# A data-dependent branch moved in a fused two-block transformer: its tiles, its place, and the loads ahead of it

## The chip, the cores and the metric

The kernel runs on one core of a Trainium2 chip. The metric is the device time of one execution in microseconds, the median of several runs. The engines are TensorE (PE, its weight loads PEld), VectorE (DVE), ScalarE (ACT), GpSimd (POOL) and SyncE (SP), which here issues the weight transfers.

## The reference

One sequence of 256 tokens with 1024 features, float32, goes through two blocks. The first block is a layer norm, an adaptive modulation, a mixing layer (latent attention beside an RWKV recurrence) and a mixture of experts; the second block is two layers of feed-forward, mixing (three kinds of heads) and feed-forward. The change touches the mixture of experts alone:

```python
logits = (ht @ router_w + router_b)
top_val, top_idx = lax.top_k(logits, 4)            # 4 of 32 experts for each token
gates = jax.nn.softmax(top_val, axis=-1)
u = clamped_swiglu(h_rows @ w1[e] + b1[e])         # w1[e]: 1024 x 2048
y = u @ w2[e] + b2[e]                              # w2[e]: 1024 x 1024
out[token] += gate * y
```

Every expert has a row count that depends on the data; 256 tokens by 4 choices over 32 experts are 32 rows in the mean.

## The kernel before, in words

The program is unrolled. A scheduler that works from a timeline simulation puts the instructions of each engine in order ahead of time; each engine then runs its own list and waits on semaphores. Instructions inside a conditional block are not mixed with those outside it.

The experts are worked in 16 pairs (`moe`, line 1255 and on). Each expert has 64 slots, so that a pair fills 128 rows. For each pair `gather` (L1152 and on) builds a one-hot of the pair's tokens (`oh`, VectorE), its gated form (`go`, GpSimd), picks the rows on TensorE (16 matmuls `m<-oh,xx`), evicts them into `xg` (VectorE and ScalarE in turn) and transposes `go` into `GT`. Then come the first layer (`p` or `s` `<-w,xg`, in two halves f of 1024 columns), transposes and the clamped SwiGLU into `u0` and `u1`, the second layer (`<-w,u`), the scaling into `y`, and the product of `GT` and `y` (`m<-y,GT`) that is added to `acc`. The gather of pair pr + 1 is written between the first and the second layer of pair pr, and the scheduler places it earlier still.

The weights come in 1 MB tiles: 16 of the first layer and 8 of the second for each pair, 24 x 16 = 384 in all, each by one SyncE transfer (`wtile`, L158). They go to buffers of 2 rings with 6 and 10 buffers, which the mixture of experts uses as one ring of 16 (`slot_tile`, L161): tile i waits until the users of tile i - 16 are done. A tile of the first layer may be loaded ahead (`prefetch`). SyncE's transfers take eight semaphores (lanes) in turn, named DMAHW0 to DMAHW7 in the order. After the experts `block2_buffers` takes buffers of the same rings for the second block, and loads and splits the first feed-forward weights.

An expert may be chosen by more than 64 tokens. `router` keeps the largest count in `over`; `moe_rest` holds a branch (`values_load` L1344, `tc.If` L1345) that is entered only where `over` is above 64, and then works every expert over all tokens. The branch stands ahead of pair 4, and its working tiles are four buffers of the ring:

```python
if pr == 4:
    self.prefetch(pr, 11)
    self.moe_rest()
```

Of the kernel before, what the change touches and what calls it, by code (L numbers as in the profile page):

```python
# [26 lines left out]
RING2 = 10  # L27
MAGIC = 12582912.0
# [5 lines left out]
# ---------------------------------------------------------------- constants  # L34
def const_arrays():
    """Arrays that depend on shapes alone: identity, masks, selections, frequencies."""
# [6 lines left out]
    a["zero"] = np.zeros((128, 128), f)   # ahead of the causal mask: queries of the second tile  # L43
# [28 lines left out]
def const_arrays2():  # L72
# [9 lines left out]
    perm = np.zeros((128, 128), f)        # [source, destination]  # L82
# [25 lines left out]
# the turns of a mixing layer: tiles of the input projection and streams of work  # L108
# [3 lines left out]
# the turns of the first block's streams of work  # L112
# [3 lines left out]
class K:  # L116
# [12 lines left out]
    # ------------------------------------------------------------ helpers  # L129
# [5 lines left out]
    def banks(self, ctx, **tags):  # L135
        """PSUM banks by stream; streams with banks of their own can run ahead of one another."""
        self.psp = ctx.enter_context(self.tc.tile_pool(name="ps", bufs=1, space=PSUM))
        self.psn = tags
# [22 lines left out]
    def slot_tile(self, which=0):  # L161
        """The next 1 MB buffer of the weight stream; in the mixture of experts it has both rings."""
        if self.ring_i is not None:
            which = int(self.ring_i % (RING + RING2) >= RING)
            self.ring_i += 1
        return self.t(self.rings[which], [128, 2048], "w")

    def rsqrt(self, pool, x, n, scale=1.0, eps=0.0, floor=None, tag="rs", eng=None):
        """x [128, n] -> 1/sqrt(x * scale + eps), three Newton steps on the vector engine."""
# [20 lines left out]
    def split(self, hi, lo, src, hi_eng="s", lo_eng="v"):  # L190
        """src (float32) = hi + lo exactly, both of the short float32r form."""
        nc = self.nc
        if hi_eng == "s":
            nc.scalar.copy(hi, src)  # L194
        elif hi_eng == "v":
            nc.vector.tensor_copy(hi, src)
        else:
            nc.gpsimd.tensor_copy(hi, src)
        (nc.vector if lo_eng == "v" else nc.gpsimd).tensor_tensor(lo, src, hi, op=OP.subtract)  # L199
# [7 lines left out]
    def conv_slot(self, w, ring=1, n=1024, **kw):  # L207
        """[128, n] of weights, split into a buffer of a ring."""
# [10 lines left out]
    def bcast_T(self, out, col):  # L219
        """out[p, t] = col[t, 0] for t in the 128 partitions of col."""  # L220
        self.mm(out, col.to_broadcast([128, 128]), self.ident)

    # ------------------------------------------------------------ block 1
# [14 lines left out]
    def load_rows(self, name, items, pool, queues):  # L238
        """Rows of 128 from the small vectors."""
# [7 lines left out]
    def to_cols(self, name, rows, pool):  # L247
        """Rows of 128 to columns over the partitions."""
# [7 lines left out]
    def phase_a(self, ctx):  # L256
# [6 lines left out]
        # ---- first loads  # L263
# [31 lines left out]
        # ---- silu(c), spread to 32 columns for the matrix-vector products  # L295
# [9 lines left out]
        # ---- embedding layer norm (tokens on partitions), transposed  # L305
# [27 lines left out]
        # ---- h = LN(x) (1 + scale) + shift by chunks of features, each as soon as its columns of the modulation are  # L333
        # there, and the rows of w_in that meet it (the columns of RWKV), into seven banks
# [40 lines left out]
        # token shift  # L375
# [5 lines left out]
        # residual alpha * x, features on partitions, in place  # L381
# [90 lines left out]
        # the streams of work and the order in which they take turns  # L472
# [12 lines left out]
        # residual and layer norm 1 (tokens on partitions), logits of the router from the sums before the norm  # L485
# [62 lines left out]
    def ln_stats2(self, pool, parts):  # L548
        """Of two token tiles: (mean, variance) [128, 2, 2], 1 / sqrt(variance + eps) and minus mean times that [128, 2]."""
# [17 lines left out]
    def matvec(self, p, w):  # L567
        """Four partial sums of silu(c) @ w in rows 0, 32, 64, 96 of p."""
# [4 lines left out]
    def ada_pair(self, j, ws):  # L573
        """Columns 2 j, 2 j + 1 of the first two sections of modT, [128, 48] = silu(c) @ ada_w + ada_b."""
# [12 lines left out]
    def ada_tile(self, sec, j, w, tag):  # L587
        """Columns 2 j, 2 j + 1 of a section of modT."""
# [10 lines left out]
    def mla(self, M, ml, sq, qlat, kvl, krot, cosT, sinT, wqn, wqr, wuk, wuv):  # L599
        """Latent attention: norms, rotary parts, values.  # L600
        Yields after every group of matrix products that the vector engines have to follow."""
# [7 lines left out]
        # rms norms of the two latents  # L609
# [22 lines left out]
        # rotary parts  # L632
# [29 lines left out]
    def mla_heads(self, ml, cs, tag, n, oT):  # L662
        """Two heads for each chunk in cs: operands [96, 2, T], scores, softmax, values."""
# [54 lines left out]
    def mla_end(self, ml, oT):  # L718
# [5 lines left out]
        # rms norm over all heads  # L724
# [16 lines left out]
    def softmax(self, t, e, p, H, S_, scale, mask):  # L741
        """p [128, H * S_] scores in PSUM -> normalised rows in SBUF."""
# [15 lines left out]
    def rwkv(self, hh, tag, wa, wg):  # L758
        """RWKV-7 for the four heads of channel chunks 2 hh and 2 hh + 1; the result replaces r in Z.
        Yields after every group of matrix products that the vector engines have to follow."""  # L760
# [7 lines left out]
        # twelve working pieces of [128, 512], in three of the weight stream's buffers  # L768
        bufs = [self.slot_tile(1) for _ in range(3)]
        raw = lambda i: bufs[i // 4][:, (i % 4) * 512:(i % 4) * 512 + 512]  # L770
        q2 = lambda i: raw(i).rearrange("p (c t) -> p c t", c=2)                    # features on partitions
        n4 = lambda i: raw(i).rearrange("p (a h s) -> p a h s", a=2, h=4)           # tokens on partitions
# [9 lines left out]
        # decay and in-context rate  # L782
# [19 lines left out]
        # kk = normalised k * k_k ; k' = k (1 + (a - 1) k_a)  # L802
# [36 lines left out]
        def blocks(lhs, rhs, par, p, o0=0):  # L839
            # [64, 64] per (tile, head, chunk parity) on partitions parity * 64 + row;  # L840
            # the two head parities are two row tiles of the array: a bank for each
# [15 lines left out]
        # inverse of I + strictly lower, by doubling of the diagonal blocks, 32 wide  # L857
# [11 lines left out]
        def coupling(n):  # L869
            # the rows of level n that couple the halves of its diagonal blocks  # L870
# [21 lines left out]
        RbkT = bufs[0][:, 1024:2048].rearrange("p (x s) -> p x s", s=64)            # b and b1 are spent  # L892
# [3 lines left out]
        def others():  # L896
            # the rest of the operands, between the steps of the inverse
# [15 lines left out]
            # tokens-on-partitions copies: [128, tile, 4 heads, 64]  # L913
# [24 lines left out]
        # last doubling to 64: X = V22 A21 V11  # L938
# [12 lines left out]
        # Y0 = A_ak V  # L951
# [15 lines left out]
        # chunk by chunk: U = -T (kk S^T + Y0) ; S^T <- e^bC S^T + a^ U + k^ V  # L967
# [35 lines left out]
        # outputs, tokens on partitions, group norm per head  # L1003
# [26 lines left out]
        # back to features on partitions; affine, bonus, gate  # L1030
# [21 lines left out]
    # ------------------------------------------------------------ mixture of experts  # L1052
    def row_of(self, out, cols, k0, n):
        """out[p, 128 i + j] = cols[j, k0 + i] on every partition (PSUM)."""
# [3 lines left out]
    def router_prep(self, Ro):  # L1058
        """h = xn1 * A2 + B2; router weights scaled by A2 with their column sums, and the constant part of the logits."""
# [25 lines left out]
    def router(self, Ro, plg, mv, rs, space):  # L1085
        """Top 4 of 32, gates, slot of every token in each of its experts; space: two of [128, 256]."""
# [59 lines left out]
    def one_hot(self, oh, pr):  # L1146
        """Of a pair of experts: oh[t, a, (expert, slot)] = 1 where the token sits."""
# [4 lines left out]
    def gather(self, Mo, pr):  # L1152
        """Rows of a pair of experts: xg [128 d, 8, (expert, slot)] and the gated one-hot [(expert, slot), T]."""
# [26 lines left out]
        else:  # L1180
            # the first pair takes its rows as they come
# [16 lines left out]
    def swiglu_clamped(self, gl, ln, th, pg, pl, bg, bl, u, flat=lambda x: x):  # L1198
        """u = 2 * min(g, 7) sigmoid(1.702 min(g, 7)) (clip(l, -7, 7) + 1), g and l in PSUM plus biases."""
# [9 lines left out]
    def moe_bias1(self, Mo):  # L1209
        """First-layer biases as columns: [j, (glu 8 | lin 8), expert]."""  # L1210
# [9 lines left out]
    def moe_base(self, Mo):  # L1220
        """The sum over experts starts as alpha * x1 + (1 + gt2) * (gates @ b2), tokens on partitions."""
# [34 lines left out]
    def moe(self, Mo, B):  # L1256
# [6 lines left out]
        for pr in range(self.pairs):  # L1263
            if pr == 4:
                self.prefetch(pr, 11)
                self.moe_rest()
# [34 lines left out]
            if pr + 1 < N_EXP // 2:  # L1301
                nxt = self.gather(Mo, pr + 1)
            last = pr == N_EXP // 2 - 1
            if last:
                # the sum so far goes ahead into the banks that take the last pair's part
# [18 lines left out]
            for a in range(2):  # L1324
                for d in range(2):
# [5 lines left out]
                    V.tensor_tensor(o, o, p, op=OP.add)  # L1331

    def moe_rest(self):
        """Tokens past an expert's 64 slots: every expert over all tokens, gated; only entered when there are any."""
# [4 lines left out]
        u, h2T = r3(self.slot_tile(), 8), r3(self.slot_tile(), 8)  # L1339
        wt, tm = self.slot_tile(), self.slot_tile()  # L1340
        tmps = [tm[:, i * T:(i + 1) * T] for i in range(4)]
        og, sel, bc = r3(tm[:, 1024:1088], 2), r3(tm[:, 1088:1152], 2), r3(tm[:, 1152:1168], 8)
        cnt, gc = tm[:, 1168:1169], tm[:, 1169:1171]
        rv = nc.values_load(self.over[0:1, 0:1], min_val=0, max_val=T)  # L1344
        with tc.If(rv > SLOTS):  # L1345
            for k in range(8):
# [3 lines left out]
                V.tensor_scalar(h2T[:, k], p[:, :T], self.A2[:, k:k + 1], self.B2[:, k:k + 1], op0=OP.mult, op1=OP.add)  # L1350
            V.scalar_tensor_tensor(og, self.slot, SLOTS - 0.5, self.gate, op0=OP.is_gt, op1=OP.mult)
            V.memset(cnt, 0.0)
            with tc.For_i(0, N_EXP, 1) as e:
# [6 lines left out]
                for f in range(4):  # L1360
                    ph = [ps("p") for _ in range(2)]
                    for k in range(8):
                        w = wt[:, (k % 2) * 512:(k % 2) * 512 + 512]
                        nc.sync.dma_start(w, I["exp_w1"][0, bass.ds(e, 1), k * 128:(k + 1) * 128, f * 512:(f + 1) * 512].rearrange("o p c -> p (o c)"))
                        for j in range(2):
                            for s in range(2):
                                mm(ph[j][:, s * T:(s + 1) * T], w[:, j * 256 + s:(j + 1) * 256:2], h2T[:, k], k == 0 and s == 0, k == 7)
                    for j in range(2):
                        c_ = f * 2 + j
                        self.swiglu_clamped(*tmps[:3], ph[j][:, :T], ph[j][:, T:], bc[:, c_, 0:1].to_broadcast([128, T]),  # L1370
# [558 lines left out]
```

## Time and profile before

| | us |
|---|---|
| median of 3 runs | 2356.72 |
| lowest and highest run | 2351.95, 2367.12 |
| span of the profiled execution | 2349.5 |
| PE busy | 2273.6 (97%) |
| DVE busy | 1174.8 (50%) |
| ACT busy | 719.5 (31%) |
| POOL busy | 159.8 (7%) |
| weights of the experts | 384 transfers of 1024 KB |

The span goes from the first to the last instruction of one profiled execution; for that execution no device time is given apart from its span. Matmul ends are modelled, so a busy TensorE is not one at its peak. A matmul in float32 appears as two records. The trace shows none of the instructions inside the branch: with the inputs used here it is not entered.

### The profile page before, as it was taken

What the parts mean: (1) busy time and instruction counts of PE and PEld (TensorE: products, weight loads), DVE (VectorE), ACT (ScalarE), POOL (GpSimd) and SP (SyncE); (2) the same over time, 40 slices, a digit from 0 to 9 for tenths busy, and PEclk for the clock granted to TensorE, in tenths of its full rate; (3) what the DMA queues carried; (4) which work ended last, traced back from release to release, by engine and by line L of the source; (5) the groups of instructions that cost most, each with busy time, mean ns of one, the idle gap of its engine ahead of it and who ended that gap; (6) DMA issues with size and microseconds to landing.
All of it is one profiled execution on the core that took longest, in us unless ns stands there. A gap on an engine that the chain in (4) does not pass through costs nothing.

```text
span 2349.5 us, 37821 instructions
## 1 busy us (share of the span) xinstructions
PE 2273.6 (97%) x15957; PEld 1641.7 (70%) x15957; DVE 1174.8 (50%) x2233; ACT 719.5 (31%) x1186; POOL 159.8 (7%) x189
## 2 busy tenths in 40 slices
PE   7999899999999999999997999999999999999998
PEld 6777643343344434333334999999999999999998
DVE  5758332221222222212214666896667666897664
ACT  4423111110000000000003444654444444655443
POOL 3310100000000000000002000120001000121000
PEclk9879999999999999999999999999999999999999
DMA  9625899999999999999997554534555655535550
GB/s 322 187 74 187 312 397 383 391 403 362 399 408 401 406 408 407 409 408 409 409 409 275 198 183 159 180 108 146 186 190 163 197 180 162 180 102 169 188 188 19
DMA packets 275967, 626.46 MB, mean 267 GB/s; under 512 B 14576, under 2 KB 160368, under 8 KB 275760
## 3 DMA queue, kind: packets, MB, share of 16 engines
q1 hardware_dynamic: 274240, 621.38, 72.4%
q8 instruction: 127, 2.08, 0.4%
q0 software_dynamic: 1264, 2.08, 0.3%
q10 hardware_dynamic: 288, 0.52, 0.1%
q14 instruction: 48, 0.39, 0.0%
HBM read 622.89 MB, written 1.05 MB: 266 GB/s over the span
## 4 chain that ended last, share of the span: by engine, by line
PE 67%; DMA 8%; DVE 2%; ACT 1%; issue 0%; DVEq 0%; ACTq 0%
PE p L148 22%; PE s L148 21%; PE m L148 15%; DMA w<-in_exp_w_dram 8%; PE r L148 8%; PE r L1288 1%; DVE w L199 0%; PE r L1289 0%; ACT w L1489 0%; DVE w L1490 0%; PE s L1728 0%; PE m L1195 0%; DVE xx L1525 0%; DVE l2y L178 0%; DVE l2x L179 0%
## 5 line engine op out<-in xcount | busy, mean ns | idle before, releaser
L199 DVE TENSOR_TENSOR w<-w,w 128x1024 fp32r<-128x1024 f32 (+2 forms) x360 | 439.3, 1229 | 265.7 <-ACT w L194 265.7
L194 ACT CAST w<-w 128x1024 fp32r<-128x1024 f32 (+2 forms) x364 | 375.2, 1041 | 455.2 <-PE m L148 254.1
L148 PE MATMUL s<-w,w 128*128 128x256 f32 (+1 forms) x2392 | 305.1, 279 | 4.5 <-ACT w L194 4.5
L148 PE MATMUL m<-w,w 128*128 128x256 f32 (+1 forms) x2240 | 303.1, 284 | 5.2 <-DVE w L199 2.0
L148 PEld LDWEIGHTS s<-w,w 128*128 128x128 f32 (+1 forms) x2392 | 286.0, 187 | 6.8 <-ACT w L194 4.6
L148 PEld LDWEIGHTS m<-w,w 128*128 128x128 f32 (+1 forms) x2240 | 281.6, 191 | 9.1 <-DVE w L199 2.6
L148 PE MATMUL p<-w,xg 128*64 128x512 f32 x1024 | 266.3, 602 | 8.2 <-PEq L1345 7.2
L148 PE MATMUL s<-w,xg 128*64 128x512 f32 x1024 | 267.2, 598 | 0.0
L148 PE MATMUL p<-w,w 128*128 128x256 f32 x1728 | 228.6, 288 | 0.0
L148 PEld LDWEIGHTS p<-w,w 128*128 128x128 f32 x1728 | 214.6, 192 | 7.7 <-issue 5.6
L148 PEld LDWEIGHTS p<-w,xg 128*64 128x64 f32 x1024 | 89.4, 138 | 157.1 <-issue 135.2
L148 PEld LDWEIGHTS s<-w,xg 128*64 128x64 f32 x1024 | 89.7, 136 | 146.8 <-issue 137.3
L1201 DVE TENSOR_TENSOR ag<-r,b1T 128x512 f32<-128x512 f32 x32 | 22.1, 691 | 297.4 <-PE r L1288 297.4
L1174 ACT ACTIVATE xg<-m,B,A 128x128 f32<-128x128 f32 x62 | 28.3, 457 | 412.7 <-DVE xg L1176 408.5
L148 PE MATMUL p<-w,u 128*64 128x512 f32 x512 | 133.3, 599 | 5.1 <-DMA w<-in_exp_w_dram 4.8
L148 PE MATMUL s<-w,u 128*64 128x512 f32 x512 | 129.1, 598 | 4.9 <-DMA w<-in_exp_w_dram 4.9
L148 PEld LDWEIGHTS p<-w,u 128*64 128x64 f32 x512 | 45.6, 136 | 85.4 <-issue 68.2
L148 PEld LDWEIGHTS s<-w,u 128*64 128x64 f32 x512 | 44.0, 136 | 83.0 <-issue 66.8
L1513 POOL TENSOR_TENSOR w<-w,th 128x256 f32<-128x256 f32 x47 | 40.9, 870 | 840.8 <-ACT th L1511 839.2
L1176 DVE TENSOR_SCALAR xg<-m,A,B 128x128 f32<-128x128 f32 x62 | 25.4, 409 | 135.4 <-PE m L148 125.7
L148 PEld LDWEIGHTS m<-oh,xx 128*128 128x128 f32 x496 | 59.9, 196 | 28.8 <-issue 27.6
L1331 DVE TENSOR_TENSOR acc<-acc,m 128x512 f32<-128x512 f32 x60 | 41.3, 688 | 65.7 <-PE m L148 65.7
(722 smaller groups left out, 2718.2 us busy)
## 6 DMA issues: line engine op xcount, KB each, us to landing
w<-in_exp_w_dram SPq DMA_DIRECT2D x384, 1024.0 KB, 18.5
w<-in_ffn_w_gate_dram SPq DMA_DIRECT2D x44, 1024.0 KB, 5.4
w<-in_ffn_w_up_dram SPq DMA_DIRECT2D x44, 1024.0 KB, 5.4
w<-in_ffn_w_down_dram SPq DMA_DIRECT2D x44, 1024.0 KB, 4.9
w<-in_w_in_dram SPq DMA_DIRECT2D x29, 1024.0 KB, 5.6
w<-in_ada_w_dram SPq DMA_DIRECT2D x24, 1024.0 KB, 6.1
w<-in_w_out_dram SPq DMA_DIRECT2D x8, 1024.0 KB, 4.9
w<-in_w_in_dram SPq DMA_DIRECT2D x8, 896.0 KB, 10.7
```

Source lines behind the costliest of these rows:

```text
L148: return self.nc.tensor.matmul(out, lhsT, rhs, start=start, stop=stop, skip_group_check=True, **kw)
L194: nc.scalar.copy(hi, src)
L199: (nc.vector if lo_eng == "v" else nc.gpsimd).tensor_tensor(lo, src, hi, op=OP.subtract)
L1174: S.activation(xg[:, d], p[:, j * 128:(j + 1) * 128], AF.Identity, scale=self.A2[:, d:d + 1], bias=self.B2[:, d:d + 1])
L1176: V.tensor_scalar(xg[:, d], p[:, j * 128:(j + 1) * 128], self.A2[:, d:d + 1], self.B2[:, d:d + 1], op0=OP.mult, op1=OP.add)
L1201: V.tensor_tensor(gl, pg, bg, op=OP.add)
L1288: PE.transpose(pg[:, o], h[:, j * 256:(j + 1) * 256:2], self.ident)
L1331: V.tensor_tensor(o, o, p, op=OP.add)
L1513: G.tensor_tensor(q[:, 0], q[:, 0], sq, op=OP.add)
```

## The change

Four things are changed together. The branch now stands at the end of pair 3 (`REST = 3`), behind its sums. All 16 first-layer tiles of pair 4 are loaded ahead of it, not 11. The gather of pair 4 is written behind the branch. The body of the branch works in tiles of the pair's own tags (`h`, `xg`, `u0`, `u1`, `y`, `ag`, `al`, `at`, `oh`), not in four ring buffers; its instructions are the same otherwise. Comments are gone throughout, and the line numbers differ by a few (the loads' L158 is L160, the branch's L1345 is L1356).

```diff
+REST = 3
...
         for pr in range(self.pairs):
-            if pr == 4:
-                self.prefetch(pr, 11)
-                self.moe_rest()
             xg, GT = nxt
...
-            if pr + 1 < N_EXP // 2:
+            if pr + 1 < N_EXP // 2 and pr != REST:
                 nxt = self.gather(Mo, pr + 1)
...
+            if pr == REST:
+                self.prefetch(pr + 1, 16)
+                self.moe_rest(Mo)
+                nxt = self.gather(Mo, pr + 1)
...
-    def moe_rest(self):
+    def moe_rest(self, Mo):
...
-        u, h2T = r3(self.slot_tile(), 8), r3(self.slot_tile(), 8)
-        wt, tm = self.slot_tile(), self.slot_tile()
-        tmps = [tm[:, i * T:(i + 1) * T] for i in range(4)]
-        og, sel, bc = r3(tm[:, 1024:1088], 2), r3(tm[:, 1088:1152], 2), r3(tm[:, 1152:1168], 8)
-        cnt, gc = tm[:, 1168:1169], tm[:, 1169:1171]
+        hs = [r3(t(Mo, [128, D], "h", bufs=2), 4) for _ in range(2)]
+        xs = [t(Mo, [128, 8, 128], "xg", bufs=2).rearrange("p a b -> p (a b)") for _ in range(2)]
+        u = [h[:, c] for h in hs for c in range(4)]
+        h2T = [x[:, c * T:(c + 1) * T] for x in xs for c in range(4)]
+        w1s = [t(Mo, [128, 4, 128], n).rearrange("p a b -> p (a b)") for n in ("u0", "u1")]
+        w2s = t(Mo, [128, D], "y")
+        t4 = lambda n, **k: t(Mo, [128, 4, 2, 64], n, **k).rearrange("p a b c -> p (a b c)")
+        ta, tb, tmp = t4("ag", bufs=2), t4("al"), t4("at")
+        tmps = [ta[:, 0:T], ta[:, T:], tb[:, 0:T]]
+        tm = t(Mo, [128, 2, 2, 64], "oh", bufs=2).rearrange("p a b c -> p (a b c)")
+        og, sel, bc = r3(tm[:, 0:64], 2), r3(tm[:, 64:128], 2), r3(tm[:, 128:144], 8)
+        cnt, gc = tm[:, 144:145], tm[:, 145:147]
         rv = nc.values_load(self.over[0:1, 0:1], min_val=0, max_val=T)
         with tc.If(rv > SLOTS):
...
-                        w = wt[:, (k % 2) * 512:(k % 2) * 512 + 512]
+                        w = w1s[k % 2]
...
-                    w = wt[:, 1024:2048]
+                    w = w2s
```

What this moves in the order of the engines, with the numbers that tell tiles apart (`w_684_4453` is a ring buffer's tile; `in_exp_w1_dram` and `in_exp_w2_dram` are the experts' first and second layer; the rows of the branch's body, which is not run, are left out at "..."). SyncE at the branch, before: the last two of pair 4's eleven early loads, the branch, and the loads that follow it.

```order
L158 DMA w_683_4451<-in_exp_w1_dram 128x2x1024 [waits DMAHW0_49,PE_49]
L158 DMA w_684_4453<-in_exp_w1_dram 128x2x1024 [waits DMAHW1_49,PE_49]
L1345 COMPARE_AND_BRANCH
...
L1345 UNCONDITIONAL_BRANCH [waits DMAHW0_49,DMAHW1_49,DMAHW2_49,DMAHW3_49,DMAHW4_49,DMAHW5_49,DMAHW6_49,DMAHW7_49]
L158 DMA w_720_4870<-in_exp_w1_dram 128x2x1024 [waits DMAHW3_49,PE_49]
L158 DMA w_721_4880<-in_exp_w1_dram 128x2x1024 [waits DMAHW2_49,DMAHW4_49,DVE_49,Activation_49]
```

SyncE at the same place in the change: the last two of pair 4's sixteen first-layer loads, the branch, and what follows it.

```order
L160 DMA w_681_4423<-in_exp_w1_dram 128x2x1024 [waits DMAHW5_49,PE_49]
L160 DMA w_682_4425<-in_exp_w1_dram 128x2x1024 [waits DMAHW6_49,PE_49]
L1356 COMPARE_AND_BRANCH
...
L1356 UNCONDITIONAL_BRANCH [waits DMAHW0_49,DMAHW1_49,DMAHW2_49,DMAHW3_49,DMAHW4_49,DMAHW5_49,DMAHW6_49,DMAHW7_49]
L160 DMA w_748_4975<-in_exp_w2_dram 128x2x1024 [waits DMAHW0_49,PE_49]
L160 DMA w_749_4977<-in_exp_w2_dram 128x2x1024 [waits DMAHW1_49,PE_49]
```

Five first-layer loads moved from behind the branch to ahead of it; the first load behind it is now one of pair 4's second layer. The eight waits at the end of the branch are the same.

TensorE at the branch, before: the last sum of pair 3, the branch, and the first layer of pair 4, with the gather of pair 5 (`oh_732`) between.

```order
L148 MATMUL m_673_4430<-y_669_4418,GT_601_4112 128x512
L1344 TENSOR_LOAD over_408_3229
L1345 COMPARE_AND_BRANCH
...
L1345 UNCONDITIONAL_BRANCH
L148 MATMUL p_709_4802<-w_674_4433,xg_654_4336 64x512
L148 MATMUL p_709_4802<-w_675_4435,xg_654_4336 64x512
```

TensorE at the same place in the change: `oh_714` is the one-hot of pair 4, `xg_716` its rows.

```order
L150 MATMUL m_666_4392<-y_662_4380,GT_601_4112 128x512
L1355 TENSOR_LOAD over_408_3229
L1356 COMPARE_AND_BRANCH
...
L1356 UNCONDITIONAL_BRANCH
L150 MATMUL m_717_4788<-oh_714_4781,xx_382_3113 128x128
L150 MATMUL m_718_4801<-oh_714_4781,xx_382_3113 128x128
L150 MATMUL m_717_4788<-oh_714_4781,xx_382_3113 128x128 x7
L150 MATMUL m_718_4801<-oh_714_4781,xx_382_3113 128x128 x7
L150 MATMUL p_721_4819<-w_667_4395,xg_716_4787 64x512
```

The gather of pair 4 left its old place between the first matmuls of pair 3 and now stands directly behind the branch, ahead of pair 4's first layer. From pair 5 on, and in everything after the experts, the rows are the same but for the numbers of tiles and lines.

## Rows read from the trace of the kernel before

**Rows 1.** Busy time by stage: busy us (records) of each engine, clock, DMA share, rate.
```profile
core 0: us, PE busy (x) PEld busy (x) DVE busy (x) ACT busy (x) POOL busy (x), PEclk, DMA share, GB/s
480.00:525.00 45.00, 45.00 (x198) 18.18 (x194) 11.29 (x21) 5.76 (x9) 0.76 (x2) 1.00 1.03 408
525.00:540.00 15.00, 7.83 (x33) 3.54 (x33) 0.69 (x1) 0.00 (x0) 0.00 (x0) 0.77 0.66 201
540.00:740.00 200.00, 199.95 (x863) 83.15 (x863) 45.48 (x88) 19.92 (x37) 3.02 (x8) 1.00 1.02 404
740.00:1240.00 500.00, 490.00 (x1998) 195.94 (x1994) 103.02 (x189) 42.20 (x77) 4.27 (x15) 1.00 1.02 408
```

**Rows 2.** The chain of waits, 720 to 1330 us: start, us, what.
```profile
742.29 18.61 DMA w<-in_exp_w_dram
...
805.89 18.60 DMA w<-in_exp_w_dram
...
1238.32 18.60 DMA w<-in_exp_w_dram
```

**Rows 3.** The page's DMA issues: count, KB of each, median us from issue to landing.
```profile
w<-in_exp_w_dram SPq DMA_DIRECT2D x384, 1024.0 KB, 18.5
```

**Rows 4.** Instructions in order of time: start, us, engine and line, count of records, idle.
```profile
473.58 2.27 PE L148 MATMUL m<-oh,xx 128*128 128x128 f32 x18
...
477.65 1.83 PE L148 MATMUL m<-oh,xx 128*128 128x128 f32 x14
...
482.98 0.44 PE L1195 MATMUL m<-ident,go 128*128 128x128 f32 x2
...
507.19 14.01 PE L148 MATMUL s<-w,u 128*64 128x512 f32 x64
...
520.55 0.65 PE L148 MATMUL s<-w,u 128*64 128x512 f32 x2
...
532.19 5.25 PE L148 MATMUL p<-w,xg 128*64 128x512 f32 x16 [7.17 <-PEq L1345]
...
541.52 0.41 DVE L1176 TENSOR_SCALAR xg<-m,A,B 128x128 f32<-128x128 f32 x1 [15.78 <-PE m L148]
```

**Rows 5.** Line L1345, the branch: ns min/median/max, first and last start in us.
```profile
L1345 SPq EVENT_SEMAPHORE  x8: 17/17/17, 531.4 to 534.4; - x8
...
L1345 SPq COMPARE_BRANCH  x1: 53/53/53, 517.1 to 517.1; - x1
L1345 PEldq COMPARE_BRANCH  x1: 7392/7392/7392, 524.5 to 524.5; - x1
L1345 DVEq COMPARE_BRANCH  x1: 72/72/72, 525.7 to 525.7; - x1
L1345 DVEq EVENT_SEMAPHORE  x1: 21/21/21, 526.3 to 526.3; - x1
L1345 PEldq EVENT_SEMAPHORE  x1: 51/51/51, 531.9 to 531.9; - x1
```

**Rows 6.** SyncE's transfers around the branch in order of time.
```profile
514.30 2.74 SPq L158 DMA_DIRECT2D w<-in_exp_w_dram  x1
...
534.52 1.46 SPq L158 DMA_DIRECT2D w<-in_exp_w_dram  x3
```

**Rows 7.** Busy time in short windows behind the branch, columns as in rows 1.
```profile
530.00:532.00 2.00, 0.00 (x0) 0.00 (x0) 0.00 (x0) 0.00 (x0) 0.00 (x0) 0.50 0.47 182
...
534.00:536.00 2.00, 2.00 (x10) 0.62 (x8) 0.00 (x0) 0.00 (x0) 0.00 (x0) 0.64 0.21 37
536.00:538.00 2.00, 2.00 (x13) 0.91 (x10) 0.00 (x0) 0.00 (x0) 0.00 (x0) 1.00 0.88 229
538.00:540.00 2.00, 2.00 (x13) 1.34 (x13) 0.00 (x0) 0.00 (x0) 0.00 (x0) 1.00 0.97 225
```

**Rows 8.** Waits from 380 to 526 us: us in total, times, longest.
```profile
PEld p L148 <- DMA w<-in_exp_w_dram: 3.1, 6, 0.8
```

**Rows 9.** The end of the experts: SyncE's first feed-forward load, the rate, its split.
```profile
1248.96 0.37 SPq L158 DMA_DIRECT2D w<-in_ffn_w_gate_dram  x1
...
1250.00:1256.00 6.00, 6.00 (x28) 2.25 (x24) 0.00 (x0) 0.00 (x0) 0.00 (x0) 1.00 1.02 368
1256.00:1260.00 4.00, 3.35 (x12) 1.08 (x12) 0.21 (x1) 0.14 (x1) 0.00 (x0) 1.00 0.96 287
...
1259.86 1.99 ACT L194 CAST w<-w 128x1024 fp32r<-128x1024 f32 x2 [16.03 <-DMA w<-in_ffn_w_gate_dram]
```

**Rows 10.** DMA queues from 529 to 530 us: packets, MB, share.
```profile
q8 instruction: 1, 0.02, 6.8%
```

More of the change, by code (lines that the diff above doesn't have):

```diff
@@ L1349, in moe_rest @@
                     PE.transpose(p[:, a * 128:(a + 1) * 128], self.xn1[:, a, k * 128:(k + 1) * 128], self.ident)
-                V.tensor_scalar(h2T[:, k], p[:, :T], self.A2[:, k:k + 1], self.B2[:, k:k + 1], op0=OP.mult, op1=OP.add)
+                V.tensor_scalar(h2T[k], p[:, :T], self.A2[:, k:k + 1], self.B2[:, k:k + 1], op0=OP.mult, op1=OP.add)
             V.scalar_tensor_tensor(og, self.slot, SLOTS - 0.5, self.gate, op0=OP.is_gt, op1=OP.mult)
@@ L1366, in moe_rest @@
                             for s in range(2):
-                                mm(ph[j][:, s * T:(s + 1) * T], w[:, j * 256 + s:(j + 1) * 256:2], h2T[:, k], k == 0 and s == 0, k == 7)
+                                mm(ph[j][:, s * T:(s + 1) * T], w[:, j * 256 + s:(j + 1) * 256:2], h2T[k], k == 0 and s == 0, k == 7)
                     for j in range(2):
                         c_ = f * 2 + j
-                        self.swiglu_clamped(*tmps[:3], ph[j][:, :T], ph[j][:, T:], bc[:, c_, 0:1].to_broadcast([128, T]),
-                                            bc[:, c_, 1:2].to_broadcast([128, T]), u[:, c_])
+                        self.swiglu_clamped(*tmps, ph[j][:, :T], ph[j][:, T:], bc[:, c_, 0:1].to_broadcast([128, T]),
+                                            bc[:, c_, 1:2].to_broadcast([128, T]), u[c_])
                 yp = [ps("r"), ps("r"), ps("s"), ps("s")]
                 for fc in range(8):
-                    w = wt[:, 1024:2048]
+                    w = w2s
                     nc.sync.dma_start(w, I["exp_w2"][0, bass.ds(e, 1), fc * 128:(fc + 1) * 128, :].rearrange("o p c -> p (o c)"))
@@ L1377, in moe_rest @@
                         for d in range(2):
-                            mm(yp[a * 2 + d], u[:, fc, a * 128:(a + 1) * 128], w[:, d * 512:(d + 1) * 512], fc == 0, fc == 7)
+                            mm(yp[a * 2 + d], u[fc][:, a * 128:(a + 1) * 128], w[:, d * 512:(d + 1) * 512], fc == 0, fc == 7)
                 for a in range(2):
@@ L1382, in moe_rest @@
                         o = self.acc[:, a, s]
-                        tmp = tm[:, 0:512]
                         V.tensor_tensor(tmp, yp[a * 2 + d], self.g2row[:, s], op=OP.mult)
```

## The prediction

> **What bounds the kernel now.** I read the stages first (busy time and DMA rate by window), then the chain of waits in the expert stage, then the branch itself, line by line on each engine. The windows show one stage, from 480 to 1240 us, in which the DMA share stands at its ceiling (1.02 to 1.03) at 404 to 408 GB/s, with a single hole: 525 to 540, at 201 GB/s [rows 1]. TensorE reads 97% and more there, but its ends are modelled, so that proves nothing. The chain does: from 742 us on, once in every pair, it runs back over a weight load of 18.6 us, next to the 18.5 that a load of this stage takes from issue to landing in the median [rows 2, 3]. So the experts' weights are bound by the rate of the transfers. One load of 1024 KB is 1.0486 MB, at 408 GB/s 2.57 us; TensorE needs 64 records in 14.01 us for 8 loads, 1.75 us each [rows 4], and has time to catch up. What a change in this stage is worth is therefore what it does to the transfers' holes: a late TensorE costs nothing unless it holds up a load.
>
> The hole is the branch. It is not taken (no instruction of its body is in the trace), yet it costs (408 - 201) / 408 x 15 us = **7.6 us** of transfers [rows 1]. Its course: SyncE issues the eleventh load of pair 4 at 514.30 and compares at 517.1; then it passes eight semaphore instructions, the first at 531.4, the last at 534.4; the next load starts at 534.52 [rows 5, 6]. The order's row at the end of the branch names what the eight wait for, DMAHW0 to DMAHW7, one for each lane of SyncE's DMAs: SyncE drains its own queue. That fits: from 517.0, when the eleventh load was in, to 534.4 are 17.4 us, about the 18.5 of a load. TensorE jumps at 524.5, needs 7.39 us for that one instruction and starts again at 532.19 [rows 4, 5], at half its clock, 1.2 GHz, until about 535.4 [rows 7]. But it is not TensorE that makes the hole: the loads stop because SyncE stands still until the last one has landed.
>
> **The change, part by part.**
>
> *Five loads go ahead of the branch* (16 in place of 11, SyncE). Their buffers come free with pair 3's second-layer tiles, the last at 521.2 [rows 4], less 4.5 (next part); the queue takes one load each 2.57 us, so it and not the buffers is the limit: the sixteenth goes in at 517.0 + 5 x 2.57 = 529.9. SyncE then compares there and drains as before: last landing 534.4 + 12.9 = 547.3. The same eight waits stand behind the branch, and the next load needs the same time to get going. The hole is **moved by 12.9 us, not closed: 0**. Of its 7.6 us some are a slow refill, 225 GB/s still at 538 to 540 [rows 7]; about 4 us at that rate lose 4 x (408 - 225) / 408 = 1.8 us. That part may go or double, so this term is 0, between -1.8 and +1.8.
>
> *The gather of pair 4 goes behind the branch* (one-hot on VectorE, `go` on GpSimd, 16 matmuls, two transposes, evictions). In the profile it lay between pair 3's first matmuls: 2.27 + 1.83 + 0.44 = 4.5 us [rows 4]. TensorE hardly waited for loads there (3.1 us in the whole stretch from 380 to 526) [rows 8], so it comes to the branch 4.5 us earlier: 520.0. It pays 7.39 for the jump, 0.3 to the first matmul: 527.7. VectorE, which passes the branch from 525.7 to 526.3 [rows 5], has the one-hots ready by then; GpSimd's `go` feeds only the two transposes, which stand behind the first ten matmuls of pair 4. The 32 records of the gather cost 4.1 us at full clock; at half clock for the first 3.2 us (as from 532.19 to 535.4) they take 3.2 + 2.5 = 5.7: 533.4. One eviction of 0.41 us [rows 4] and as much again for its semaphores: 534.2. The first 16 records use up the first two loads in 3.5 us: 537.7. This is the first moment at which a load behind the branch finds a buffer, and SyncE asks at 547.3: **9.6 us of cover**. By 547.3 TensorE has done 9.6 - 4.1 (gather of pair 5) = 5.5 us more, three loads at 1.75, so about five buffers are free, as many as stood unfilled before. Cost 0. If the cover were gone, each us of a later TensorE would widen the hole by one.
>
> *The body works in a pair's tiles*. As it is never run, its own work is nothing in both kernels. New waits that the scheduler could have set for these tiles stand inside the body; behind it every engine waits as before, by the rows of the order.
>
> *Four ring buffers fewer are taken*: 391 in all become 387 (24 x 16 loads, two biases, one table, four for the branch). The ring turns by 16, so the stage ends four places earlier in it. The first feed-forward load waited in the profile for a buffer of pair 15's second layer and was issued at 1248.96 only; the transfers dip to 368 and 287 GB/s [rows 9], (6 x 40 + 4 x 121) / 408 = 1.8 us. In the new place that load takes a buffer of the ninth first-layer tile, free long before, and can follow the last expert load directly. The splits that wait for it start at 1259.86, and what follows waits on the layer norm as well, so I take **-0.5**, between -1.8 and 0.
>
> **Sum**: 0 + 0 + 0 - 0.5. The profiled span is 2349.5 us; the median of the three runs, 2356.72, lies 7.2 above it, the fastest 2.5 above. I put the sum on the median: **2356 us**, with a range of its own of 2353 to 2358.5 from the terms, and 2350 to 2362 with what medians of so few runs move (the three cover 15 us).
>
> **Rivals.** *The hole closes (faster).* The loads needed for pair 4 are all ahead of the branch, so one might read the 7.6 us as time in which SyncE waited for the branch's ring buffers. Then it goes: 2356.7 - 7.6 = 2349. Against it: SyncE passes the branch at the moment when its own loads have landed, and the eight waits are there word for word. Chance 0.08.
>
> *TensorE's jump grows (slower).* The 7.39 us is the time of a code load: in 529 to 530 one packet of 0.02 MB moves on the instruction queue [rows 10], and TensorE goes on at 531.9. In the profile the loads were running dry then; in the change they are not. If the code queues behind the loads that are in at 520.0, 18.5 us of them, TensorE restarts at 538.8 and gives its first buffers at 548.8: +1.5. If it waits until all sixteen have landed, 547.3 + 0.5 and then 0.3 + 5.7 + 0.8 + 3.5 = 558.1: +11, 2368. It decides once the jump takes more than 7.4 + 9.6 = 17.0 us. Against it: the packet passed about 5 us ahead of the last landing, at 534.4, so it does not go to the end of the line. Chance 0.12 for anything from +1.5 to +11.
>
> The Trainium skill, DMA: Bandwidth & Descriptors (Queues, rings and completion order), says that each DMA engine takes turns between the queues it has work for, a packet at a time. By that rule the code would not stand behind all the loads, the jump would stay near 7 us under full load too, and this rival would add nothing; the packet that overtook the last loads agrees. By the other reading, one line for all, the sum would be up to 2368.
>
> *Something else*, a transfer disturbed elsewhere or a chip that differs: 0.05. The forecast keeps 0.75.
>
> **Numbers.** A measurement of this kernel can tell about 1%, 23.6 us, from no change; that is three times the whole hole. Within 1%: 0.95; faster 0.02 and slower 0.03 are left to what I have not seen. The range takes in the closed hole and its jitter below, and nearly all of the slow jump above: 2348 to 2367.
>
> **What would show it.** SyncE's compare near 530, its eight semaphores ending near 547, the next load directly behind; a hole of about 7.6 us in the DMA rate from there on, and full rate from 480 until then. TensorE's jump near 520 and about 7 us long, then the gather's matmuls at half clock, then pair 4's first layer near 534. In the last pair the first gate load is issued before 1245. I am wrong if the rate shows no hole (SyncE did not drain), if the jump is over 17 us, or if the first load behind the branch waits for TensorE and not for the lanes.

## The result, and the profile after

| | before | changed |
|---|---|---|
| median of 9 runs, us | 2356.72 | 2375.70 |
| lowest and highest run | 2351.64, 2368.24 | 2364.00, 2382.36 |
| ratio, 95% interval | 1 | **1.0061** [1.0039, 1.0084] |
| span of the profiled execution | 2349.5 | 2377.6 |
| cast of the largest count to first layer-norm statistics, us | 989.7 | **1004.9** |

The ratio is worth 14.4 us and its interval 9.2 to 19.8; the two medians of the table stand 19.0 us apart, inside it. The change made the kernel slower, by about twice the hole that the branch cost before, and the measured median lies above the predicted range.

The two spans differ by 28.1 us, and only about half of that is the change's. The mixing stage of the first block, long before the branch, ran at another granted clock in the two executions. Of the windows of both kernels (columns as in [rows 1]), before:

```profile
100.00:150.00 50.00, 47.71 (x908) 36.59 (x900) 32.98 (x74) 10.52 (x23) 17.58 (x16) 0.74 0.24 81
```

and changed:

```profile
100.00:150.00 50.00, 49.76 (x666) 37.59 (x668) 28.19 (x69) 6.68 (x14) 13.27 (x12) 0.50 0.22 76
```

Unchanged instructions ran there at a mean clock of 0.74 and of 0.50, and what follows starts later; that the clock of this window is the whole cause is not shown. So I measure a length inside each trace: from the cast of the largest count (`over`), which ends the router, to the first layer-norm statistics behind the experts (`bst`). The rows of those two tiles, before:

```profile
L1132 DVE CAST over<-most x1: 143/143/143, 272.0 to 272.0; 128x1 int32<-128x1 f32 x1
...
L555 DVE BATCH_NORM_STATS2 bst<-r x2: 698/698/699, 1261.7 to 1263.4; 128x6 f32<-128x512 f32 x2
```

and changed:

```profile
L1134 DVE CAST over<-most x1: 143/143/143, 286.4 to 286.4; 128x1 int32<-128x1 f32 x1
...
L557 DVE BATCH_NORM_STATS2 bst<-r x2: 698/699/700, 1291.3 to 1293.0; 128x6 f32<-128x512 f32 x2
```

1261.7 - 272.0 = 989.7, and 1291.3 - 286.4 = 1004.9: **15.2 us more**, beside the 14.4 of the ratio. As far as one profile of each tells, the whole loss lies between these two points. The rest of the spans' difference is the 286.4 - 272.0 = 14.4 us by which the cast came later, less 1.5 us behind the statistics; that this 14.4 equals the ratio's is chance. Taken off a time of the changed trace, these 14.4 us set it beside one of before.

The transfers in the changed kernel, by stage:

```profile
525.00:540.00 15.00, 9.15 (x34) 3.75 (x31) 4.63 (x8) 0.00 (x0) 0.75 (x2) 0.90 1.03 404
540.00:560.00 20.00, 6.43 (x30) 6.05 (x28) 0.00 (x0) 0.00 (x0) 0.00 (x0) 0.50 0.96 366
560.00:580.00 20.00, 17.72 (x60) 6.36 (x61) 2.78 (x9) 1.72 (x4) 1.51 (x4) 0.81 0.53 200
580.00:600.00 20.00, 20.00 (x82) 8.30 (x81) 5.25 (x13) 3.63 (x7) 0.76 (x2) 1.00 0.78 277
600.00:740.00 140.00, 140.00 (x615) 59.47 (x613) 33.07 (x61) 12.66 (x23) 1.51 (x4) 1.00 1.02 399
740.00:1240.00 500.00, 491.64 (x2022) 202.48 (x2024) 106.90 (x198) 43.45 (x80) 4.53 (x12) 1.00 1.02 406
```

Against 408 GB/s the three windows from 540 to 600 lose (42 + 208 + 131) x 20 / 408 = 18.7 us, and the last two 3.1 and 2.5. The kernel before lost 7.6 from 525 to 540, and 2.0 (404 for 200 us) from 540 to 740 [rows 1]. The difference, 24.3 - 9.6 = 14.7 us, is close to the 15.2 of the length: the stage is still bound by the transfers, and its hole has grown.

Next, the branch's line in the changed kernel, which answers to [rows 5] (ns, first and last start), with who waited for it:

```profile
L1356 SPq EVENT_SEMAPHORE  x8: 17/17/17, 550.6 to 561.3; - x8
...
L1356 PEldq COMPARE_BRANCH  x1: 6063/6063/6063, 532.7 to 532.7; - x1
...
L1356 SPq COMPARE_BRANCH  x1: 53/53/53, 545.1 to 545.1; - x1
...
  DVE oh L1151: 26.9, 2
```

SyncE compares at 545.1 and settles its eighth lane at 561.3 (to settle a lane is to wait for its own loads to land and then to count the transfers of the skipped body on it as made); less 14.4 that is 530.7 and 546.9, where the prediction had 529.9 and 547.3. TensorE jumps at 518.3 by the clock of before, for 6.06 us. The drain and the jump are as forecast. The last row is new: one-hots on VectorE wait 26.9 us, in two waits, for the branch's semaphores. The timeline of the changed kernel (columns as in [rows 4]) shows what stands behind it:

```profile
534.60 0.49 DVE L1151 TENSOR_TENSOR oh<-iota,slot 128x128 f32<-128x128 f32 x2 [0.62 <-DVEq L1356]
...
539.10 3.75 PE L150 MATMUL m<-oh,xx 128*128 128x128 f32 x16 [5.84 <-PEq L1356]
545.42 3.57 PE L150 MATMUL m<-oh,xx 128*128 128x128 f32 x16 [2.57 <-issue]
561.40 0.49 DVE L1151 TENSOR_TENSOR oh<-iota,slot 128x128 f32<-128x128 f32 x2 [26.31 <-SPq L1356]
561.82 0.40 DVE L1178 TENSOR_SCALAR xg<-m,A,B 128x128 f32<-128x128 f32 x1
...
562.28 8.01 PE L150 MATMUL p<-w,xg 128*64 128x512 f32 x20 [13.28 <-DVE xg L1178]
```

Read it from the end: TensorE starts pair 4's first layer at 562.28, 13.28 us late, on the evictions `xg`. Their sums were done at 549.0, but the evictions stand behind a one-hot in VectorE's list, and that one-hot, of pair 5 and needed by nobody yet, starts when SyncE settles its last lane. The order of the changed kernel on VectorE says why (`oh_714` is pair 4's one-hot, `oh_739` pair 5's):

```
L1356 UNCONDITIONAL_BRANCH [waits DVE_49]
L1151 TENSOR_TENSOR oh_714_4781<-iota_337_2687,slot_403_3209 128x128 [waits Pool_49]
L1151 TENSOR_TENSOR oh_714_4781<-iota_337_2687,slot_403_3209 128x128
L1151 TENSOR_TENSOR oh_739_4935<-iota_337_2687,slot_403_3209 128x128 [waits DMAHW7_49,DVE_49]
L1151 TENSOR_TENSOR oh_739_4935<-iota_337_2687,slot_403_3209 128x128
L1178 TENSOR_SCALAR xg_716_4787<-m_717_4788,A2_333_2660,B2_334_2661 128x128 [waits PE_49]
```

The branch's small tile `tm` now has the tag `oh`, with two buffers: `tm` takes one, pair 4's one-hot the other, pair 5's again that of `tm`. A part of `tm`, the bias `bc`, is loaded in the body by SyncE on lane 7. Pair 5's one-hot must not write before that load is done, so it waits for DMAHW7. The load is never made, and the one-hot starts 0.1 us after SyncE has passed its last lane.

SyncE's next transfers, each row a few issues (start, us from the first to the last, count):

```profile
568.60 0.91 SPq L160 DMA_DIRECT2D w<-in_exp_w_dram  x2
...
573.42 1.21 SPq L160 DMA_DIRECT2D w<-in_exp_w_dram  x2
...
580.59 1.21 SPq L160 DMA_DIRECT2D w<-in_exp_w_dram  x2
...
588.23 1.19 SPq L160 DMA_DIRECT2D w<-in_exp_w_dram  x2
```

SyncE is free from 561.3 and finds no buffer until 568.6. Then TensorE frees two in 7.2 to 7.6 us, where two loads take 5.1: it starts with nothing ahead, and works pieces of pair 5's gather between.

### The profile page after: what moved, and what is told of

Same layout as the page of the kernel before. It is cut to its first block, busy times and chain, and to the rows that moved or that the text cites. A ratio compares the mean times of both kernels' runs of the same rounds, so it can differ in the third digit from the quotient of the medians.

```text
span 2377.6 us, 37825 instructions
## 1 busy us (share of the span) xinstructions
PE 2290.3 (96%) x15957; PEld 1661.4 (70%) x15957; DVE 1174.5 (49%) x2233; ACT 719.0 (30%) x1186; POOL 161.0 (7%) x189
## 4 chain that ended last, share of the span: by engine, by line
PE 64%; DMA 7%; DVE 3%; ACT 1%; issue 1%; DVEq 0%; ACTq 0%
PE s L150 21%; PE p L150 20%; PE m L150 14%; PE r L150 7%; DMA w<-in_exp_w_dram 7%; DVE w L201 1%; PE r L1287 1%; PE r L1288 0%; ACT w L1499 0%; PE s L1738 0%; PE m L1197 0%; ACT w L196 0%; DVE w L1500 0%; DVE AT L1804 0%; DVE xx L1535 0%
## 5 line engine op out<-in xcount | busy, mean ns | idle before, releaser
L150 PE MATMUL p<-w,xg 128*64 128x512 f32 x1024 | 269.3, 605 | 14.5 <-DVE xg L1178 13.3
L1283 ACT COPY h<-s 128x512 f32<-128x512 f32 x32 | 18.7, 585 | 199.2 <-PE s L150 199.2
```

Source lines behind the costliest of these rows:

```text
L150: return self.nc.tensor.matmul(out, lhsT, rhs, start=start, stop=stop, skip_group_check=True, **kw)
L1283: S.copy(h[:, nb * 512:(nb + 1) * 512], hp[nb])
```

## Experiments

**Theory 1**: VectorE's one-hot waits for SyncE's drained lane and holds up the evictions behind it. **Theory 2**: the gather in its new place is late by itself, from TensorE's jump and the half clock behind it. **Theory 3**: sixteen loads ahead make the drain dearer. All ratios are to the kernel before, measured beside each run; lengths are from the cast to the statistics, each from one profile.

| | ratio, 95% interval | length, us |
|---|---|---|
| before | 1 | 989.7 |
| changed | 1.0061 [1.0039, 1.0084] | 1004.9 |
| bias in its own buffer | 1.0008 [0.9988, 1.0028] | 989.0 |
| all small tiles in their own | 0.9992 [0.9970, 1.0013] | 988.5 |
| the place alone | 0.9988 [0.9968, 1.0007] | 990.7 |
| three one-hot buffers | 1.0075 [1.0051, 1.0099] | 1004.5 |
| changed, body's transfers by GpSimd | 0.9990 [0.9967, 1.0013] | 987.3 |
| the same, small tiles in their own | 0.9978 [0.9960, 0.9997] | 984.7 |
| before without the branch | 0.9972 [0.9952, 0.9993] | 981.7 |
| before, body's transfers by GpSimd | 0.9971 [0.9951, 0.9991] | 983.6 |
| before with two branches | 1.0031 [1.0010, 1.0052] | 1001.8 |

**The bias in its own buffer.**

```diff
-        og, sel, bc = r3(tm[:, 0:64], 2), r3(tm[:, 64:128], 2), r3(tm[:, 128:144], 8)
+        og, sel, bc = r3(tm[:, 0:64], 2), r3(tm[:, 64:128], 2), r3(t(Mo, [128, 16], "bc", bufs=1), 8)
```

> The changed kernel, with one tile taken out of the shared one-hot buffer: the branch's 16 columns of bias, the only part of that buffer that SyncE's transfers write, get a buffer of their own. VectorE's instructions behind the branch keep their order. The time is compared by the ratio to the kernel before and by the length from the cast of the largest count to the first layer-norm statistics behind the experts (before 989.7 us, changed 1004.9). Theory 1 (in the change, the one-hot of pair 5 waits for SyncE's lane to be drained, since its buffer is one that the branch loads; the evictions of pair 4's rows stand behind it): VectorE no longer waits for SyncE there, TensorE's wait of 13.3 us ahead of pair 4's first layer goes, buffers are free when SyncE asks: length 988 to 993 us, ratio 0.999 to 1.002. Theory 2 (the gather behind the branch is itself what is late: TensorE's jump and 32 records at half clock): nothing changes, 1003 to 1007 us, ratio 1.006. Theory 3 (sixteen loads ahead make the drain dearer): nothing changes either, 1.006.

Measured: 1.0008 and 989.0. Moving 16 columns gives all of it back, with the same place, the same sixteen loads and the same list on VectorE. Two rows of VectorE's timeline, and two short windows:

```profile
519.71 1.33 DVE L1151 TENSOR_TENSOR oh<-iota,slot 128x128 f32<-128x128 f32 x4 [0.63 <-DVEq L1356]
530.61 0.41 DVE L1178 TENSOR_SCALAR xg<-m,A,B 128x128 f32<-128x128 f32 x1 [9.57 <-PE m L150]
```

```profile
540.00:545.00 5.00, 5.00 (x22) 2.26 (x22) 0.00 (x0) 0.00 (x0) 0.00 (x0) 1.00 0.70 281
545.00:550.00 5.00, 5.00 (x18) 1.82 (x19) 0.41 (x1) 0.33 (x1) 0.00 (x0) 1.00 0.55 175
```

Both one-hots run at once, and the evictions wait for TensorE alone. Counted from the cast (at 271.9 here) the first eviction starts at 258.7, in the changed kernel at 561.82 - 286.4 = 275.4: 16.7 us later there, with a length 15.9 us greater. The hole of the drain is still here, in 540 to 550, as a hole moved but not grown. Theories 2 and 3 fall.

The branch's line here, then pair 4's first layer on TensorE and SyncE's first loads behind the branch:

```profile
L1356 SPq EVENT_SEMAPHORE  x8: 17/17/17, 535.2 to 546.1; - x8
...
L1356 PEldq COMPARE_BRANCH  x1: 6123/6123/6123, 517.8 to 517.8; - x1
```

```profile
532.06 5.36 PE L150 MATMUL p<-w,xg 128*64 128x512 f32 x20
```

```profile
546.23 3.14 SPq L160 DMA_DIRECT2D w<-in_exp_w_dram  x6
```

Six loads go out one after the other once the last lane is settled, into buffers that TensorE freed while SyncE stood still; in the changed kernel only two go at first, and 7.3 us after the last lane. TensorE's first 20 records of pair 4 also take 5.36 us here and 8.01 there, where TensorE came out of its 13.28 us of waiting at the lower clock, 1.2 GHz (0.50 granted in the window from 540 to 560). So the wait made TensorE later by up to 2.6 us more, through the clock.

**All small tiles in a buffer of their own.**

```diff
-        tm = t(Mo, [128, 2, 2, 64], "oh", bufs=2).rearrange("p a b c -> p (a b c)")
+        tm = t(Mo, [128, 256], "bt", bufs=1)
```

> The changed kernel, with all the small tiles of the branch (gates, selection, bias, count) in a buffer of their own, no longer in a one-hot's. Both one-hots behind the branch can then go ahead of it, and VectorE starts behind the branch with the evictions of pair 4's rows. Theory 1 (the one-hot's wait for SyncE's lane): as in the run with only the bias apart, length 988 to 993 us from the cast of the count to the layer norm, ratio 0.999 to 1.002; the earlier one-hots bring nothing more, since TensorE's jump lets the gather start only near 518 + 6 us. Theories 2 and 3 (place of the gather, number of loads ahead): 1003 to 1007 us, ratio 1.006.

Measured: 0.9992 and 988.5, as expected of theory 1: one-hots ahead of the branch win nothing that can be told from the run above.

**The place alone**: ring buffers for the body as before, eleven loads ahead.

```diff
-                self.prefetch(pr + 1, 16)
+                self.prefetch(pr + 1, 11)
...
-        hs = [r3(t(Mo, [128, D], "h", bufs=2), 4) for _ in range(2)]
...
+        uu, hh = r3(self.slot_tile(), 8), r3(self.slot_tile(), 8)
+        wt, tm = self.slot_tile(), self.slot_tile()
...
```

> The place alone: the branch stands behind pair 3 with the gather of pair 4 behind it, as in the change, but its body works in four buffers of the ring and eleven loads stand ahead of it, as in the kernel before. Theory 1 (the one-hot's wait for SyncE's lane): no one-hot shares a buffer with the branch, so length 988 to 994 us, ratio 0.999 to 1.002. Theory 2 (the gather behind the branch is late by itself, from TensorE's jump and the half clock): 1000 to 1007 us, ratio 1.005 or more. Theory 3 (the sixteen loads): as theory 1.

Measured: 0.9988 and 990.7. The gather behind the branch costs nothing that can be told, with eleven loads ahead as, by the run with the bias apart, with sixteen.

**Three buffers for the one-hots.**

```diff
-        oh, go = t(Mo, [128, 2, 2, 64], "oh", bufs=2) if pr else self.oh0, t(Mo, [128, 2, 2, 64], "go", bufs=2)
+        oh, go = t(Mo, [128, 2, 2, 64], "oh", bufs=3) if pr else self.oh0, t(Mo, [128, 2, 2, 64], "go", bufs=2)
...
-        tm = t(Mo, [128, 2, 2, 64], "oh", bufs=2).rearrange("p a b c -> p (a b c)")
+        tm = t(Mo, [128, 2, 2, 64], "oh", bufs=3).rearrange("p a b c -> p (a b c)")
```

> The changed kernel with three buffers for the one-hots and the branch's small tiles, not two. In VectorE's order the one-hots of pairs 4 and 5 then wait for no lane, but that of pair 6 takes the buffer that the branch loads, waits for lane 7 of SyncE's DMAs, and stands ahead of the evictions of pair 4's rows too. Theory 1 (what stands behind a wait for the lane on VectorE): nothing is won, VectorE stands until SyncE's eighth semaphore, length 1002 to 1007 us from the cast of the count to the layer norm, ratio 1.005 to 1.007. If the cost were a shortage of buffers for one-hots, or the sharing with pair 5's one-hot as such, the third buffer would remove it: 988 to 993 us, ratio 1.000.

Measured: 1.0075 and 1004.5, as slow as the change. One more buffer does not help, since the scheduler runs one more one-hot ahead and so meets the same wait at the same place. VectorE's timeline:

```profile
534.12 1.32 DVE L1151 TENSOR_TENSOR oh<-iota,slot 128x128 f32<-128x128 f32 x4 [0.63 <-DVEq L1356]
560.66 0.49 DVE L1151 TENSOR_TENSOR oh<-iota,slot 128x128 f32<-128x128 f32 x2 [25.22 <-SPq L1356]
561.07 0.40 DVE L1178 TENSOR_SCALAR xg<-m,A,B 128x128 f32<-128x128 f32 x1
```

Four records, the one-hots of pairs 4 and 5, run at once; the third one-hot waits 25.22 us, and the evictions come behind it.

**The body's transfers by GpSimd, the small tiles still in a one-hot's buffer.** The same edit is made for the two transfers of weights in the body.

```diff
-                nc.sync.dma_start(bc, I["exp_b1"][0, bass.ds(e, 1), :].rearrange("o (c j s) -> j (o c) s", c=8, s=2))
+                nc.gpsimd.dma_start(bc, I["exp_b1"][0, bass.ds(e, 1), :].rearrange("o (c j s) -> j (o c) s", c=8, s=2))
...
```

> The changed kernel, the small tiles still in a one-hot's buffer, but the three transfers of the branch's body issued by GpSimd and not by SyncE; the body is not entered. VectorE's order is that of the change, and the one-hot of pair 5 still waits for a transfer's semaphore ahead of the evictions, now one of GpSimd's queue, which has nothing under way. Theory 1 (the wait is long only because SyncE drains its full queue before it settles the lane): the wait is below 1 us, and so is SyncE's at the branch, length 981 to 986 us, ratio 0.996 to 0.999, as with GpSimd's transfers and own small tiles. If a wait of this kind for a transfer that is not made costs by itself, or GpSimd settles late: 990 to 1005 us, ratio 1.000 to 1.006.

Measured: 0.9990, inside what was expected, and 987.3, a little over it. The loss is gone, though VectorE's list still has the one-hot with a transfer's semaphore, now one of GpSimd's queue, at the same place. The branch's line and VectorE's timeline:

```profile
L1356 POOLq EVENT_SEMAPHORE  x4: 17/43/43, 418.3 to 419.8; - x4
...
L1356 SPq COMPARE_BRANCH  x1: 53/53/53, 537.6 to 537.6; - x1
```

```profile
527.21 1.32 DVE L1151 TENSOR_TENSOR oh<-iota,slot 128x128 f32<-128x128 f32 x4 [0.62 <-DVEq L1356]
537.78 0.41 DVE L1178 TENSOR_SCALAR xg<-m,A,B 128x128 f32<-128x128 f32 x1 [9.25 <-PE m L150]
```

GpSimd had settled its semaphores at 419.8, over 100 us before VectorE asked, and SyncE has no semaphore row at the branch at all. So what cost 15 us was not a wait for a transfer that is never made, but whose queue settles it, and when.

**The same with the small tiles in a buffer of their own.** The two edits above together.

> The changed kernel with the small tiles in a buffer of their own and the three transfers of the branch's body issued by GpSimd, not by SyncE; the body is not entered. Theory 1 and the reading of the hole (SyncE stands still at the branch because the branch's body issues its DMAs, whose lanes it settles at the end of the branch): SyncE then has no transfer in the body, passes the branch within 1 us, and the rate stays near 405 GB/s but for what a late TensorE costs: the sixteenth load lands near 547 and the first buffer of pair 4 is free near 538 in the profile before's time, so the hole of 7.6 us goes: length 981 to 985 us, ratio 0.996 to 0.998. If SyncE drains at any branch, whoever issues the body's transfers: 988 to 993 us, ratio 1.000. Theories 2 and 3: 1.006 or, without a drain, what TensorE's lateness leaves of it.

Measured: 0.9978 and 984.7, faster than before. Why its length is 2.6 us below that of the run above is open; one profile of each is little for that.

**Before without the branch** (`self.moe_rest()` taken out).

> The kernel before without the branch at pair 4: the part for experts with more than 64 tokens is left out (these inputs have none). It prices the branch as such in the old place. The prediction put the hole in the transfers at 7.6 us: length from the cast of the count to the layer norm 980 to 984 us (before 989.7), ratio 0.997. If the hole were given back elsewhere (TensorE at its bound), 989 us, ratio 1.000.

Measured: 0.9972 and 981.7, 8.0 us less where 7.6 was forecast. Its DMA rate holds through the place of the hole:

```profile
525.00:530.00 5.00, 5.00 (x26) 2.27 (x24) 0.00 (x0) 0.00 (x0) 0.00 (x0) 1.00 1.01 404
530.00:535.00 5.00, 5.00 (x24) 1.90 (x20) 0.69 (x1) 0.00 (x0) 0.00 (x0) 1.00 1.02 409
```

**Before, the body's transfers by GpSimd.** The three lines of the edit above, in the kernel before.

> The kernel before, the branch in its old place with its ring buffers, but the three transfers of its body issued by GpSimd. If SyncE drains only where the body has transfers of its own, it passes the branch at once and the hole of 7.6 us goes: 981 to 985 us, ratio 0.997, as without the branch, less what TensorE's jump of 7.4 us takes (no buffer is late for it, eleven loads are ahead). If SyncE drains at any branch, or if the branch's ring buffers now wait for GpSimd: 988 to 995 us, ratio 1.000 or a little above.

Measured: 0.9971 and 983.6, 6.1 us less: within what a measurement tells, as fast as with no branch. TensorE still jumps, and the transfers go on:

```profile
L1345 SPq COMPARE_BRANCH  x1: 53/53/53, 513.3 to 513.3; - x1
L1345 PEldq COMPARE_BRANCH  x1: 7232/7232/7232, 521.5 to 521.5; - x1
```

```profile
525.00:530.00 5.00, 0.87 (x2) 0.33 (x4) 0.00 (x0) 0.00 (x0) 0.00 (x0) 0.54 1.03 412
530.00:535.00 5.00, 5.00 (x22) 2.03 (x19) 0.00 (x0) 0.00 (x0) 0.00 (x0) 0.78 1.03 407
```

With the run without the branch, that settles the reading of the hole: SyncE stands still because the body holds transfers of its own. It is also a version that beats both kernels; what it costs when the branch is entered was not tried.

**Before with two branches.**

```diff
-            if pr == 4:
+            if pr in (4, 8):
```

> The kernel before with the same branch a second time, ahead of pair 8, with eleven loads ahead of it again. It doubles the price of a branch whose body issues transfers: another 7.6 us by the hole, length 996 to 999 us, ratio 1.003 to 1.004. If the hole ahead of pair 4 came from its place (the ring's start, pair 4's neighbours) and not from the drain: 989 to 991 us, ratio 1.000.

Measured: 1.0031, as expected, and 1001.8, 3 to 6 us over what was expected. The line of the two branches:

```profile
L1345 SPq EVENT_SEMAPHORE  x16: 17/17/17, 537.8 to 800.1; - x16
...
L1345 SPq COMPARE_BRANCH  x2: 45/49/53, 524.1 to 782.8; - x2
L1345 PEldq COMPARE_BRANCH  x2: 6010/6036/6062, 530.0 to 774.7; - x2
```

The second drain lasts 800.1 - 782.8 = 17.3 us, as long as the one of the kernel before, and TensorE's two jumps take 6.01 and 6.06 us. The branch has its price again in this second place. The interval of the ratio (2.4 to 12.3 us) holds the 7.6, as it holds the 12.1 by which the length grew; what the surplus in this one profile is, I leave open.

## Why the prediction was wrong

*Five loads ahead* was right: SyncE's compare at 530.7 and last lane at 546.9 by the clock of before (forecast 529.9 and 547.3), and with the bias apart a hole that is moved and not closed, length -0.7.

*The gather behind the branch* was right in what it asserts, by the place-alone run and the run with the bias apart. There the evictions start at 530.6, by a clock 0.1 us off that of before, 2.8 us earlier than the forecast 533.4, since the jump began at 517.8 and took 6.12. But its cover was counted for the first load alone. In the changed kernel a lateness of 16.7 us cost 15.9, where a cover of 9.6 would have left 7. The first load does come 7.3 us late, 568.60 against the last lane at 561.3, up to 2.6 of it by TensorE's lower clock; the rest was lost behind it. The rows of SyncE's transfers show why: TensorE then has no buffers in stock, and while it works pair 4's first layer with another gather between, it frees them more slowly than the loads go. So the sentence at the end of that term, one us for each us past the cover, was too low as well.

***The body works in a pair's tiles* is the step that failed.** It said that the new waits "stand inside the body; behind it every engine waits as before, by the rows of the order". The rows of SyncE and TensorE did; VectorE's did not. The wait for DMAHW7 on `oh_739` stood there to be read, two rows ahead of the first eviction, and the second term had even worked out the two times that it joins: evictions wanted at 533.4, lanes settled at 547.3. An eviction that comes at 547.3 is 13.9 us late, and 9.6 of cover do not pay for that: by the forecast's own times 4.3 were left, and the cover, as said, was counted too kindly. The term was sized 0 and measured 15.9 (changed, less the bias apart).

*Four ring buffers fewer* was right in its course: with the bias apart the first feed-forward load is issued at 1239.92, where it was 1248.96 [rows 9] (forecast before 1245), and its split starts at 1259.12, 0.7 us earlier (forecast 0.5).

```profile
1239.92 2.31 SPq L160 DMA_DIRECT2D w<-in_ffn_w_gate_dram  x1
...
1259.12 2.00 ACT L196 CAST w<-w 128x1024 fp32r<-128x1024 f32 x2 [16.07 <-DMA w<-in_ffn_w_gate_dram]
```

That the size agrees may be luck: the lengths of three runs that have SyncE's drain and not VectorE's wait lie between 988.5 and 990.7, further apart than 0.7.

The rivals: the hole did not close, and the jump did not grow: 6.06 us with sixteen loads under way, 7.39 with eleven that ran dry. The Trainium skill, DMA: Bandwidth & Descriptors (Queues, rings and completion order), has the DMA engines take turns between queues by the packet. The trace agrees: of the changed kernel's DMA queues from 536 to 537 us, in the jump, the instruction queue's row is

```profile
q8 instruction: 1, 0.02, 6.9%
```

and TensorE's matmuls go on at 539.10, while SyncE's loads land until 561.3. So this packet, taken for the code, did not queue behind the loads. The case that came true, a wait on a lane behind the branch on an engine other than SyncE, was among none of the named rivals. One sign of being wrong did name what it led to, a first load behind the branch that waits for TensorE and not for the lanes: it came 7.3 us after the last lane. At 0.61% the change is within 1%, the case given 0.95.

## What to carry to other kernels

A buffer that is shared with a conditional block carries the block's waits out of it, and the engine that takes the buffer next pays them even where the block is never entered. Where a change shares a tile, read the waits of that tile's next user on its own engine, and what stands behind it in that list; and count a cover for the loads after the first too. Give the transfers of a rarely entered block to a queue that is idle, or SyncE's full queue is drained at its end; what that costs where the block is entered was not measured here.

## What the runs showed of the hardware

TensorE's jump over a block that is not entered took 6.0 to 7.4 us in each of the ten traces with the branch, with the DMA rate at 408 GB/s as well as with it falling, and in the program with two branches 6.01 and 6.06. Why it took 7.23 to 7.39 in two traces and 6.0 to 6.3 in the others is open. The other engines' compares took 45 to 72 ns. Coming out of 13.28 us without work, TensorE needed 8.01 us for 20 records that took 5.36 where it had just been at work.

The granted clock from 100 to 150 us went from 0.50 to 0.74 between executions that issue the same instructions up to the cast of the count, and that cast came between 269.3 us (before, with GpSimd's transfers) and 286.4 (changed). That window alone does not settle it: at 0.50 the cast came at 279.0 in one trace and at 285.9 to 286.4 in three. Spans of this kernel differ by up to 17 us ahead of all that was changed; a length between two marks in one trace is the safer measure of a stage behind them.
